# A decoder trunk on one core: the value projection of the first mixer with 512 moving columns in two goes, in place of 256 in four

## The chip, the cores and the metric

The kernel runs on one core of a Trainium2 chip. The metric is the device time of one launch in microseconds (us), taken as the median of several runs; a difference of about 0.2% (2.5 us here) is what a measurement of this kernel can tell from no change. Engines are named as in the profile: PE is the matrix engine's matmul side and PEld its weight loads, DVE is the vector engine, ACT the scalar engine, POOL the general engine, SP the engine that issues most transfers.

## The reference

A two-layer decoder trunk over 512 tokens and a model width of 1024, all in float32. Layer 0 is a gated linear recurrence (the *first mixer* below), layer 1 differential attention; each is followed by a gated convolutional FFN. Only the first mixer is touched:

```
def hgrn2_mixer(h, w_in, w_out, g_norm, lb):
    proj = h @ w_in
    q, f, i, g = jnp.split(proj, [HG_FDIM, 2 * HG_FDIM, 3 * HG_FDIM], axis=-1)
    q = jax.nn.silu(q)
    log_f = jnp.logaddexp(jnp.log(lb), jnp.log1p(-lb) + jax.nn.log_sigmoid(f.astype(jnp.float32)))
    k = -jnp.expm1(log_f)
    ...
    def step(S, blk):
        qb, kb, vb, lfb = blk
        b = jnp.cumsum(lfb, axis=1)
        o_inter = jnp.einsum('bthk,bhkv->bthv', qb * jnp.exp(b), S)
        scores = jnp.einsum('bthk,bshk,btshk->bhts', qb, kb, decay)
        o_intra = jnp.einsum('bhts,bshv->bthv', scores, vb)
        S_new = jnp.exp(b_last)[..., None] * S + jnp.einsum('bshk,bshv->bhkv', k_dec, vb)
        return S_new, o_inter + o_intra
    ...
    o = rmsnorm(o, g_norm) * jax.nn.silu(g.astype(jnp.float32))
    return (o @ w_out).astype(h.dtype)
```

There are eight heads of width 128. The projections q, f and g are wanted channel by token; the values i (here *values*, V) are wanted token by channel, since they are summed over tokens.

## The kernel before, in words

**Products.** A float32 product is made as three matmuls of operands that are split into a high and a low part (`mm3`, L99, L100, L101). For q, f and g the weights stand in the array and 512 tokens move: eight steps of the inner dimension, so 24 matmuls of 512 columns for each head and projection. For the values the tokens stand in the array (a block of 128) and the weights move: `value` (L279). Weights come as tiles of 128 x 1024 (512 KB): `stage` (L81) lets SP transfer one into one of three buffers `wst`; `split` makes the high part on ACT (L59) and the low part on DVE (L60), into one of three pairs `whi`, `wlo`. `spare` is a fourth such pair, used later in the mixer for the output projection.

**Values before.** The 1024 value columns are made in four goes of 256, each for two heads. A go takes two weight tiles, each holding 4 steps of the inner dimension by 256 columns, and four token blocks: 4 x 8 x 3 = 96 matmuls of 256 columns. ACT moves each of the four results from PSUM into a tile `vt` of 128 x 4 x 256 (L331), of which there are two. The first go is begun in the hand-ordered opening (`begin`): the first token block whole and the second by half.

**Per head.** `prep(h)` (L334 on) turns the projections f and q into decayed queries and keys at six block sizes, on DVE and ACT. The six key tiles of a head share one set of six buffers (`KB`), so the first of them for the next head (`k1`, L346) must wait until the matmuls that read this head's `k1` are done. `intra(h)` (L416) then has these pieces on PE: *part one*, 64 small matmuls that make scores of 32-token blocks (L423, L425), further scores (L430, L434, L437) and three transposes (L445); `kv`, three products of keys and values (L450); and the *output products* (L490, L492), which read the values `vt` and the assembled scores `scd`. Between part one and the output products DVE puts the scores into place with masked copies (L468, L479), ACT copies them into `scd` (L482, L485, L487), and DVE makes the running state `S` (L454). `gate` and `readout` follow for an earlier head.

**Order.** Outside the opening no order is written by hand in this mixer: the framework lists the instructions of each engine by its own estimate when the program is built, and each engine then runs its list in that order. PSUM has four banks called `mm` (projections and values) and four called `at` (the pieces of `intra`).

Of the kernel before, what the change touches and what calls it, by code (L numbers as in the profile page):

```python
# [11 lines left out]
F32 = mybir.dt.float32  # L12
F32R = mybir.dt.float32r
I32 = mybir.dt.int32
AF = mybir.ActivationFunctionType
# [4 lines left out]
P = 128  # L20
T = 512
D = 1024
KD = D // P
NH = 8
# [12 lines left out]
class Trunk:  # L37
# [192 lines left out]
    def begin(self, xs, acc, products, raw):  # L230

        tc, nc, a = self.tc, self.nc, self.a
        v, s = nc.vector, nc.scalar
        parts = [self.weight_tiles() for _ in products]
        for k in range(KD):
            nc.sync.dma_start(self.x[k], a["x_t"][k])
            if k in PIECES:
                c = slice(k * P, PIECES[k] * P)
                nc.sync.dma_start(raw[:, :, c], a["w_fqg"][0:len(products), :, c].rearrange("n p k -> p n k"))
        staged = [self.stage(a["w_i"][0, n]) for n in range(2)]  # L240
        sqs = [acc] + [self.sp.tile([P, T], F32, tag="sq", name="sq", bufs=2) for _ in range(KD - 1)]
        tail = range(max(PIECES), KD)

        def add(n):
            v.tensor_tensor(acc, acc, sqs[n], ALU.add)

        with tc.manual_schedule(engines=ORDERED):
            warm = self.bank("at")
            for _ in range(WARM):
                nc.tensor.matmul(warm[:, 0:P], self.ones, self.ones, start=True, stop=True)  # L250
            for k in range(KD):
                xs.append(self.x_split(k, 0))
                if k in PIECES:
                    c = slice(k * P, PIECES[k] * P)
                    for n, (hi, lo) in enumerate(parts):
                        self.split(raw[:, n, c], hi[:, c], lo[:, c])
                if k < tail[0]:
                    for ps, w in zip(products, parts):
                        self.proj(ps, w, xs, [k])
                s.activation(sqs[k], self.x[k], AF.Square)  # L260
                if k > 1:
                    add(k - 1)
                if k == KD - 3:
                    self.setup_rest()
            add(KD - 1)
            proj_tail = lambda n: self.proj(products[n], parts[n], xs, tail)
            ws = []
            for n in range(2):
                proj_tail(n)
                ws.append(self.weight_split(staged[n]))  # L270
            rc = self.rms(self.sums(acc, "at"), "n0")
            proj_tail(2)
            values = [self.bank("mm"), self.bank("at")]
            self.value(values[0], xs, ws, 0, range(KD))
            self.value(values[1], xs, ws, 1, range(KD // 2))
            rb = self.rows(rc, "n0", "at")
        return rb, rc, ws, values

    def value(self, ps, xs, ws, j, ks):  # L279

        tk = slice(j * P, (j + 1) * P)
        for k in ks:
            hi, lo = ws[k // 4]
            c = slice((k % 4) * 256, (k % 4) * 256 + 256)
            self.mm3(ps[:, :256], (xs[k][0][:, tk], xs[k][1][:, tk]), (hi[:, c], lo[:, c]), k == 0, k == KD - 1)

    def hgrn(self, xs, acc, on_tile):
        tc, nc, a, sp = self.tc, self.nc, self.a, self.sp
        v, s = nc.vector, nc.scalar
        with ExitStack() as ctx:  # L290
            hp = ctx.enter_context(tc.tile_pool(name="hgrn", bufs=1))
# [3 lines left out]
            spare = [hp.tile([P, 1024], F32R, tag=f"spare{i}", name=f"spare{i}") for i in range(2)]  # L295
# [24 lines left out]
                self.proj(ps, w, xs, range(KD))  # L320
                return ps

            def values(qt):
                ws = w_i if qt == 0 else [self.weights(a["w_i"][qt, n]) for n in range(2)]
                vt = hp.tile([P, 4, 256], F32, tag="vt", name="vt", bufs=2)
                for j in range(4):
                    ps, ks = self.bank("mm") if qt or j > 1 else begun[j], range(KD)
                    if qt == 0 and j < 2:
                        ks = range(KD // 2, KD) if j else ()
                    self.value(ps, xs, ws, j, ks)  # L330
                    s.activation(vt[:, j], ps[:, :256], AF.Identity, scale=rc[:, j:j + 1])  # L331
                return vt

            def prep(h, f_ps, q_ps):  # L334
# [81 lines left out]
            def intra(h, vt, r1, r2, qs, ks, tt):  # L416
                mm = nc.tensor.matmul
# [20 lines left out]
                       qs[64][:, P * c + 64:P * c + 128], start=True, stop=True, tile_position=(0, 0))  # L438

                ch = lambda t, c: t[:, c * P:(c + 1) * P]  # L440
                vh = lambda j: vt[:, j, (h % 2) * P:(h % 2 + 1) * P]
                q128, k128 = qs[128], ks[128]
                pk = self.bank("at")
                for c in range(3):
# [58 lines left out]
            def keep(h, po):  # L503
                o = big("o", "o", 2)
                self.sq_add(oacc, po, h == 0)
                s.copy(o, po)
                return o
# [7 lines left out]
            for h in range(NH):  # L515
                if h:
                    f_ps, q_ps = project(3 * h), project(3 * h + 1)
                if h == 0:
                    gate0 = gate(0, g_ps)
                pr[h] = prep(h, f_ps, q_ps)  # L520
                if h % 2 == 0:
                    vt[h // 2] = values(h // 2)
                if h:
                    o[h - 1] = keep(h - 1, intra(h - 1, vt[(h - 1) // 2], *pr.pop(h - 1)))
                if h > 1:
                    readout(h - 2, o[h - 2], gate(h - 2, project(3 * h - 4)) if h > 2 else gate0)
                if h == 2:
                    self.bias_vector()
            gg = [gate(h, project(3 * h + 2)) for h in (NH - 2, NH - 1)]
            readout(NH - 2, o[NH - 2], gg[0])  # L530
            o[NH - 1] = keep(NH - 1, intra(NH - 1, vt[3], *pr.pop(NH - 1)))
            readout(NH - 1, o[NH - 1], gg[1])
            steps, got = self.norm_steps(oacc, "o", "at")
            self.residual(a["w_ao"], ys, KD, on_tile, lambda: got[1][0], [None] * 3 + [spare], between=steps,
# [670 lines left out]
def by_quarter(w):  # L1205
    return np.ascontiguousarray(w.reshape(2, 4, P, 4, 256).transpose(3, 0, 2, 1, 4).reshape(4, 2, P, 1024))


def score_mask():

    s = np.arange(P) % 32
    m = np.zeros((P, 144), np.int32)
    kinds = [("q", 0), ("q", 1), ("q", 2), ("q", 3), (1, 0), (2, 0), (2, 1), (3, 0), (3, 2), (3, 1)]
    for y, (i, g) in enumerate(kinds):
        for n in range(8):
            if i == "q":
                m[:, y * 8 + n] = s == 4 * n + g
            else:
                m[:, y * 8 + n] = s == 4 * n + i - 1 - g
    kinds = [(1, 0), (2, 0), (3, 0), (2, 1), (3, 1), (3, 2)]  # L1220
    for y, (i, g) in enumerate(kinds):
        for n in range(2):
            m[:, 80 + y * 8 + n * 4:80 + y * 8 + n * 4 + 4] = (s // 4 == 4 * n + i - 1 - g)[:, None]
    m[:, 128:144] = (s < 16)[:, None]
    return m
# [19 lines left out]
def pack(i):  # L1245
    hot, far = t5_buckets()
    i = {k: np.asarray(v) for k, v in i.items()}
    w_in = i["a_w_in"][0]
    q, f, iv, g = (w_in[:, n * D:(n + 1) * D] for n in range(4))
    fqg = np.stack([by_tile(f), by_tile(q), by_tile(g)], 1).reshape(24, P, D)  # L1250
    d = {
        "x_t": np.ascontiguousarray(i["x"][0].T).reshape(KD, P, T),
        "w_fqg": fqg,
        "w_i": by_quarter(iv),
        "w_ao": by_tile(i["a_w_out"][0]),
        "gains": np.stack([columns(t) for t in (i["norm_mix"][0], i["norm_ffn"][0], i["kv_norm"], i["norm_mix"][1],
                                                i["norm_ffn"][1], i["final_norm"], i["a_gnorm"][0])], 1),
        "pack": np.concatenate([
            np.eye(P, dtype=np.float32), columns(i["a_lb_logits"][0]), columns(i["a_lb_logits"][1]),
            i["ffn_conv_w"].reshape(2, 3, 2 * KF, P).transpose(3, 0, 1, 2).reshape(P, -1),  # L1260
            i["ffn_conv_b"].reshape(2, 2 * KF, P).transpose(2, 0, 1).reshape(P, -1),
            i["b_subln"][0].reshape(P, 1)], 1),
        "rel": np.concatenate([i["rel_table"], hot], 1),
        "lam": np.stack([i[k][0] for k in ("b_lam_q1", "b_lam_k1", "b_lam_q2", "b_lam_k2")], 1),
        "w_up": np.stack([by_tile(w).reshape(2, KF, P, D).transpose(1, 0, 2, 3).reshape(2 * KF, P, D)
                          for w in i["ffn_w_up"]]),
        "w_down": np.stack([by_tile(w) for w in i["ffn_w_down"]]),
        "w_kq": np.stack([by_tile(i["kv_w"][:, :D]), by_tile(i["b_w_q"][0])], 1).reshape(16, P, D),
        "w_v": by_quarter(i["kv_w"][:, D:]),
        "w_o": by_tile(i["b_w_o"][0]),  # L1270
        "c_far": far,
        "c_mask": score_mask(),
    }
    return d
# [16 lines left out]
```

## Time and profile before

| | |
|---|---|
| median of 3 runs | 1240.84 us (1240.6 to 1240.98) |
| the profiled execution | 1240.69 us, of which the span of its instructions is 1238.4 us |
| busy in the span | PE 99%, PEld 84%, DVE 68%, ACT 47%, POOL 1% |
| the first mixer | about 24 us to 257 us of the span |
| value matmuls, first mixer | 384 of 128x256, eight transfers of 512 KB of `w_i` |

A busy time counts an instruction from its start to its modelled end; matmuls overlap, so their pace is read from the distance of their starts, not from their durations. "idle before <-X" is time in which an engine stood still and the last event that ended it.

### The profile page before, as it was taken

The page shows a single profiled execution, that of the slowest core. Times are in us where ns is not written, and L with a number is a line of the kernel's source. Part 1 is how long each engine was busy: PE and PEld are TensorE (multiplying, and loading weights), DVE is VectorE, ACT ScalarE, POOL GpSimd, SP SyncE. Part 2 cuts the span into 40 slices and gives each one's busy share as a digit, 9 for nine tenths or more (in the row PEclk, how much of TensorE's full clock was granted, in tenths as well). Part 3 has the DMA queues.
Part 4 walks back from the last instruction along what each step waited for, and adds up shares of the span by engine and source line. Part 5 has one row for each costly group of instructions (what it writes and reads, how often), then busy time and mean ns, then how long its engine had stood idle before and what let it go on. Part 6 is the DMA issues. An engine that isn't in the chain of part 4 may idle for free.

```text
span 1238.4 us, 18006 instructions
## 1 busy us (share of the span) xinstructions
PE 1227.0 (99%) x6994; PEld 1040.1 (84%) x6994; DVE 840.8 (68%) x1643; ACT 578.0 (47%) x1007; POOL 10.0 (1%) x32
## 2 busy tenths in 40 slices
PE   9999999999999999999999999999999999999997
PEld 8888898888888888888888989888888888888886
DVE  6988889587777777633356787877687777762333
ACT  6564555454444444422355666655444444442223
POOL 0000000000000000000000000000000000000001
PEclk9999999999999999999999999999999999999999
DMA  6234222232333333333333322313233333323322
GB/s 233 69 86 123 86 79 60 69 119 86 102 98 89 102 101 88 92 94 97 105 88 115 91 74 79 105 65 90 85 102 102 89 98 102 91 88 96 101 85 69
DMA packets 39613, 117.46 MB, mean 95 GB/s; under 512 B 4280, under 2 KB 10216, under 8 KB 39528
## 3 DMA queue, kind: packets, MB, share of 16 engines
q1 hardware_dynamic: 38488, 115.37, 31.0%
q8 instruction: 55, 0.90, 0.3%
q10 hardware_dynamic: 1040, 0.94, 0.2%
q14 instruction: 30, 0.25, 0.1%
HBM read 112.09 MB, written 3.68 MB: 93 GB/s over the span
## 4 chain that ended last, share of the span: by engine, by line
PE 96%; DVE 1%; ACT 1%; DMA 0%; issue 0%; SPq 0%; ACTq 0%; DVEq 0%
PE mm L99 28%; PE mm L100 28%; PE mm L101 28%; PE po L1020 1%; PE sc L977 1%; PE sc L99 1%; PE sc L100 1%; PE sc L976 1%; PE sc L101 1%; PE tp L1007 1%; PE at L490 1%; PE at L423 1%; PE at L492 0%; PE at L450 0%; DMA raw<-in_w_fqg_dram 0%; PE at L437 0%
## 5 line engine op out<-in xcount | busy, mean ns | idle before, releaser
L99 PE MATMUL mm<-xh,whi 128*128 128x512 f32 x944 | 370.8, 393 | 0.4 <-ACT whi L59 0.3
L100 PE MATMUL mm<-xl,whi 128*128 128x512 f32 x944 | 368.7, 391 | 0.5 <-DVE xl L63 0.5
L101 PE MATMUL mm<-xh,wlo 128*128 128x512 f32 x944 | 367.8, 390 | 0.0
L60 DVE TENSOR_TENSOR wlo<-wst,whi 128x1024 fp32r<-128x1024 f32 (+1 forms) x172 | 206.4, 1203 | 142.8 <-ACT whi L59 140.8
L59 ACT CAST whi<-wst 128x1024 fp32r<-128x1024 f32 (+1 forms) x172 | 177.1, 1033 | 244.5 <-PE mm L100 208.3
L99 PEld LDWEIGHTS mm<-xh,whi 128*128 128x128 f32 x944 | 177.4, 188 | 37.4 <-ACT whi L59 0.9
L101 PEld LDWEIGHTS mm<-xh,wlo 128*128 128x128 f32 x944 | 177.2, 188 | 37.0 <-DVE wlo L60 0.2
L100 PEld LDWEIGHTS mm<-xl,whi 128*128 128x128 f32 x944 | 177.4, 188 | 36.8 <-DVE xl L63 2.0
L99 PE MATMUL mm<-hh,whi 128*128 128x512 f32 (+1 forms) x374 | 141.0, 377 | 0.0
L100 PE MATMUL mm<-hl,whi 128*128 128x512 f32 (+1 forms) x374 | 140.8, 377 | 0.0
L101 PE MATMUL mm<-hh,wlo 128*128 128x512 f32 (+1 forms) x374 | 140.8, 376 | 0.0
L679 DVE TENSOR_TENSOR u<-mm,rbc_f 128x512 f32<-128x512 f32 x88 | 60.2, 688 | 73.4 <-PE mm L101 73.4
L101 PEld LDWEIGHTS mm<-hh,wlo 128*128 128x128 f32 x374 | 70.4, 188 | 13.0
L100 PEld LDWEIGHTS mm<-hl,whi 128*128 128x128 f32 x374 | 70.4, 188 | 12.9
L99 PEld LDWEIGHTS mm<-hh,whi 128*128 128x128 f32 x374 | 70.4, 188 | 12.8
L59 ACT CAST hh<-c 128x512 fp32r<-128x512 f32 x44 | 27.3, 620 | 102.7 <-DVE c L690 102.7
L681 ACT ACTIVATE c<-u,pack 128x512 f32<-128x512 f32 x88 | 71.5, 817 | 7.7 <-DVE u L679 3.6
L99 PE MATMUL mm<-whi,xh 128*128 128x256 f32 x248 | 71.6, 289 | 0.0
L101 PE MATMUL mm<-whi,xl 128*128 128x256 f32 x248 | 70.2, 283 | 0.0
L100 PE MATMUL mm<-wlo,xh 128*128 128x256 f32 x248 | 70.1, 283 | 0.0
L683 DVE SCALAR_TENSOR_TENSOR c<-u,pack,c 128x512 f32<-128x512 f32 x88 | 66.1, 751 | 2.7
L682 DVE SCALAR_TENSOR_TENSOR c<-u,pack,c 128x512 f32<-128x512 f32 x88 | 65.4, 745 | 0.0
(283 smaller groups left out, 1689.0 us busy)
## 6 DMA issues: line engine op xcount, KB each, us to landing
wst<-in_w_up_dram SPq DMA_DIRECT2D x88, 512.0 KB, 3.6
wst<-in_w_down_dram SPq DMA_DIRECT2D x32, 512.0 KB, 3.5
wst<-in_w_fqg_dram SPq DMA_DIRECT2D x21, 512.0 KB, 3.7
wst<-in_w_kq_dram SPq DMA_DIRECT2D x16, 512.0 KB, 3.6
wst<-in_w_down_dram SPq DMA_DIRECT2D x16, 384.0 KB, 3.1
wst<-in_w_i_dram SPq DMA_DIRECT2D x8, 512.0 KB, 3.7
wst<-in_w_ao_dram SPq DMA_DIRECT2D x8, 512.0 KB, 4.5
wst<-in_w_v_dram SPq DMA_DIRECT2D x8, 512.0 KB, 3.6
```

The source lines that it names most:

```text
L59: i = nc.scalar.copy(hi, x)
L60: j = nc.vector.tensor_tensor(lo, x, hi.bitcast(F32), ALU.subtract)
L99: mm(out, s[0], m[0], start=start, stop=False)
L100: mm(out, s[0], m[1], start=False, stop=False)
L101: mm(out, s[1], m[0], start=False, stop=stop)
L423: mm(pa[row, c * P:c * P + 80], ks[1][:, st], r1[:, :, 8 * bk:8 * bk + 8], start=True, stop=True, tile_position=(0, 32 * g))
L490: mm(ch(po, j), vh(j), sct[:, j], start=True, stop=(j == 0))
L679: v.tensor_tensor(u[:, 2:], ps, rb, ALU.mult)
L681: s.activation(c, u[:, 2:], AF.Identity, bias=self.cb[:, layer, n:n + 1], scale=w(2))
L682: v.scalar_tensor_tensor(c, u[:, 1:T + 1], w(1), c, ALU.mult, ALU.add)
L683: v.scalar_tensor_tensor(c, u[:, 0:T], w(0), c, ALU.mult, ALU.add)
L976: mm(sc[c], qs[h][:, c, oi], ks[h][0][:, c, 0:n], start=True, stop=False)
```

## The change

Values are made in two goes of 512 columns, each for four heads. A go takes four weight tiles, each with 2 steps of the inner dimension by 512 columns, and 4 x 8 x 3 = 96 matmuls of 512 columns. The fourth weight pair of a go is `spare`. `vt` becomes 128 x 4 x 512 with one buffer in place of two of 256 (the same bytes). In the opening the first two token blocks are each begun by half. In the loop over heads, `values` now comes behind `intra` of the head before, and for heads 0 and 4 in place of 0, 2, 4 and 6. The host lays `w_i` out by halves; the bytes are the same.

```
             values = [self.bank("mm"), self.bank("at")]
-            self.value(values[0], xs, ws, 0, range(KD))
-            self.value(values[1], xs, ws, 1, range(KD // 2))
+            for j in range(2):
+                self.value(values[j], xs, ws, j, range(KD // 2))
             rb = self.rows(rc, "n0", "at")
...
         tk = slice(j * P, (j + 1) * P)
         for k in ks:
-            hi, lo = ws[k // 4]
-            c = slice((k % 4) * 256, (k % 4) * 256 + 256)
-            self.mm3(ps[:, :256], (xs[k][0][:, tk], xs[k][1][:, tk]), (hi[:, c], lo[:, c]), k == 0, k == KD - 1)
+            hi, lo = ws[k // 2]
+            c = slice(k % 2 * T, k % 2 * T + T)
+            self.mm3(ps, (xs[k][0][:, tk], xs[k][1][:, tk]), (hi[:, c], lo[:, c]), k == 0, k == KD - 1)
...
-            def values(qt):
-                ws = w_i if qt == 0 else [self.weights(a["w_i"][qt, n]) for n in range(2)]
-                vt = hp.tile([P, 4, 256], F32, tag="vt", name="vt", bufs=2)
+            def values(half):
+                ws = w_i if half == 0 else []
+                for n in range(len(ws), 4):
+                    ws.append(self.weights(a["w_i"][half, n], tiles=spare if n == 3 else None))
+                vt = hp.tile([P, 4, T], F32, tag="vt", name="vt")
                 for j in range(4):
-                    ps, ks = self.bank("mm") if qt or j > 1 else begun[j], range(KD)
-                    if qt == 0 and j < 2:
-                        ks = range(KD // 2, KD) if j else ()
-                    self.value(ps, xs, ws, j, ks)
-                    s.activation(vt[:, j], ps[:, :256], AF.Identity, scale=rc[:, j:j + 1])
+                    begun_j = half == 0 and j < 2
+                    ps = begun[j] if begun_j else self.bank("mm")
+                    self.value(ps, xs, ws, j, range(KD // 2 if begun_j else 0, KD))
+                    s.activation(vt[:, j], ps, AF.Identity, scale=rc[:, j:j + 1])
                 return vt
...
-                if h % 2 == 0:
-                    vt[h // 2] = values(h // 2)
                 if h:
-                    o[h - 1] = keep(h - 1, intra(h - 1, vt[(h - 1) // 2], *pr.pop(h - 1)))
+                    o[h - 1] = keep(h - 1, intra(h - 1, vt[(h - 1) // 4], *pr.pop(h - 1)))
+                if h % 4 == 0:
+                    vt[h // 4] = values(h // 4)
```

The lists that the framework makes of this move too. At head 3 PE's list has, between the last transposes of part one and the output products, before the change three projections in a row (the q, f and g matmuls have the token tile `xh` or `xl` first, the value matmuls the weight tile):

```order
L445 MATMUL at_1752<-pack_247,k128_1281 128x128 x3
L99 MATMUL mm_1803<-xh0_141,whi_1799 128x512
...
L450 MATMUL at_1758<-vt_924,kt_1756 128x128 x3
...
L99 MATMUL mm_1844<-xh0_141,whi_1840 128x512
...
L99 MATMUL mm_1875<-xh0_141,whi_1871 128x512
...
L490 MATMUL at_1784<-scd1_377,vt_924 128x128 x2
L492 MATMUL at_1784<-q128_1280,S_1762 128x128
```

These are 22 matmuls of 512 ahead of `kv` and 45 behind it. With the change the same place reads:

```order
L446 MATMUL at_1528<-pack_247,k128_1174 128x128 x3
L99 MATMUL mm_1674<-whi_1587,xh4_217 128x512
...
L101 MATMUL mm_1674<-spare0_96,xl7_264 128x512
L451 MATMUL at_1534<-vt_464,kt_1532 128x128 x3
L491 MATMUL at_1560<-scd1_365,vt_464 128x128 x2
L493 MATMUL at_1560<-q128_1173,S_1538 128x128
...
L426 MATMUL at_1878<-r2_1421,k4_1417 32x48
L99 MATMUL mm_1706<-xh0_141,whi_1702 128x512
```

Twelve matmuls of the second go's last token block stand ahead of `kv`, and none between `kv` and the output products; the next projections (`mm_1706`, 72 matmuls) come behind them and behind 18 matmuls of part one of head 4. ACT's list at that place is now:

```order
L486 COPY scd1_365<-at_1499 32x4x32 x2
L488 COPY scd1_365<-at_1499 64x4x64
L332 ACTIVATE vt_1595<-mm_1596,rcol_n0_297 128x512
L332 ACTIVATE vt_1595<-mm_1622,rcol_n0_297 128x512
L332 ACTIVATE vt_1595<-mm_1648,rcol_n0_297 128x512
L332 ACTIVATE vt_1595<-mm_1674,rcol_n0_297 128x512
L143 ACTIVATE sq_1569<-at_1560 128x512
```

The second go's four results leave PSUM together, behind the `scd` copies of head 3; before, each go's four results were spread around such copies, into the other of the two `vt` buffers. From the end of the mixer on, the lists of all engines are the same as before.

More of the change, by code (lines that the diff above doesn't have):

```diff
@@ L440, in intra @@
                 ch = lambda t, c: t[:, c * P:(c + 1) * P]
-                vh = lambda j: vt[:, j, (h % 2) * P:(h % 2 + 1) * P]
+                vh = lambda j: vt[:, j, h % 4 * P:(h % 4 + 1) * P]
                 q128, k128 = qs[128], ks[128]
@@ L530, in hgrn @@
             readout(NH - 2, o[NH - 2], gg[0])
-            o[NH - 1] = keep(NH - 1, intra(NH - 1, vt[3], *pr.pop(NH - 1)))
+            o[NH - 1] = keep(NH - 1, intra(NH - 1, vt[1], *pr.pop(NH - 1)))
             readout(NH - 1, o[NH - 1], gg[1])
@@ L1206, in by_quarter, with by_half @@
     return np.ascontiguousarray(w.reshape(2, 4, P, 4, 256).transpose(3, 0, 2, 1, 4).reshape(4, 2, P, 1024))
+def by_half(w):
+    return np.ascontiguousarray(w.reshape(4, 2, P, 2, T).transpose(3, 0, 2, 1, 4).reshape(2, 4, P, 1024))
 def score_mask():
@@ L1253, in pack @@
         "w_fqg": fqg,
-        "w_i": by_quarter(iv),
+        "w_i": by_half(iv),
         "w_ao": by_tile(i["a_w_out"][0]),
```

## The prediction

> **What bounds the kernel now.** I began with the page's busy times and its chain of waits.
>
> ```profile
> PE 1227.0 (99%) x6994; PEld 1040.1 (84%) x6994; DVE 840.8 (68%) x1643; ACT 578.0 (47%) x1007; POOL 10.0 (1%) x32
> PE 96%; DVE 1%; ACT 1%; DMA 0%; issue 0%; SPq 0%; ACTq 0%; DVEq 0%
> ```
>
> PE carries the end: whatever shortens PE's list shortens the kernel, as long as no new wait opens. So the second view is the waits of PE in the first mixer (20 to 260 us), and the third the busy time of all engines there in stretches.
>
> ```profile
> PE at L490 <- issue: 1.3, 1, 1.3
> ...
> 30.00:60.00 30.00, 30.00 (x270) 25.67 (x268) 29.02 (x77) 15.46 (x31) 0.00 (x0) 1.00 0.24 71
> 120.00:150.00 30.00, 30.00 (x389) 26.46 (x388) 23.66 (x62) 18.77 (x42) 0.00 (x0) 1.00 0.25 76
> ```
>
> In the second kind of row the columns are PE, PEld, DVE, ACT, POOL, granted clock, DMA share and GB/s. PE stands still only once in the mixer, 1.3 us before output products (those of head 0). But DVE is busy 29 of 30 us at the start of the mixer and 24 of 30 later, and a head's output products need what DVE makes. PE is never late because its list always holds other matmuls while DVE works. That cover is what this change rearranges, so the order matters as much as the matmuls' price.
>
> **The price of the matmuls.** Their pace is read from starts in the timeline of PE.
>
> ```profile
> 24.23 0.29 PE L99 MATMUL mm<-whi,xh 128*128 128x256 f32 x1
> ...
> 29.51 0.28 PE L101 MATMUL at<-whi,xl 128*128 128x256 f32 x1
> ...
> 36.05 0.40 PE L100 MATMUL mm<-xl,whi 128*128 128x512 f32 x1
> ...
> 39.92 0.39 PE L99 MATMUL mm<-xh,whi 128*128 128x512 f32 x1
> ```
>
> From 24.23 to 29.51 lie 44 steps between value matmuls of 256 columns: 5.28 / 44 = 0.1200 us. From 36.05 to 39.92 lie 17 steps of 512: 3.87 / 17 = 0.2276 us. Two of 256 become one of 512: 0.2400 - 0.2276 = 0.0124 us saved, 192 times, **-2.4 us**. Single steps of the second run read 0.22 to 0.24, which bounds the term at -3.8 and 0. [...]
>
> ACT moves half as many results of twice the width; it is busy about half of the time here, so that is hidden but for the place below. Eight transfers of 512 KB stay eight, all on SP. In the opening the third and fourth weight tiles are now values too.
>
> ```profile
> 22.55 4.00 SPq L81 DMA_DIRECT2D wst<-in_w_fqg_dram  x3
> 23.88 1.05 ACT L59 CAST whi<-wst 128x1024 fp32r<-128x1024 f32 x1 [1.24 <-PE mm L100]
> 24.96 1.23 DVE L60 TENSOR_TENSOR wlo<-wst,whi 128x1024 fp32r<-128x1024 f32 x1 [0.20 <-ACT whi L59]
> DMA to landing us min/median/max: 3.6/3.7/4.1
> ...
> DMA to landing us min/median/max: 3.5/3.9/7.9
> ```
>
> The third tile is split by 26.2. The fourth is issued at 22.55, lands at most 4.1 later (the landings of 20 to 40 us) at 26.7, and is split by 26.7 + 1.05 + 1.23 = 29.0. The two first halves (24 matmuls of 0.2276 from 23.9) keep PE until 29.3, and the fourth tile is wanted after seven more. Nothing waits: **0**. If the landing took 7.9 us, the longest of the first 80, PE would wait some 2 us; this is kept for the upper end.
>
> **The wait that goes.** Before head 0's output products PE has had 31 matmuls of 512 and 73 of 256 since the transposes (15.8 us) and will have 67 of 512 (15.2 us). DVE's list in that stretch loses a weight split, `qe`, `F` and the sums that follow it, and gains four short products, about 3 us less by their usual durations (an estimate). The wait of 1.3 us should vanish: **-1.3**, or 0 at the other end.
>
> **The wait that comes.** The place is head 3, with the order shown above. These rows of PE, DVE and ACT are head 3 as it is before the change.
>
> ```profile
> 126.72 0.21 PE L425 MATMUL at<-r,k 128*32 128x48 f32 x1
> 128.02 0.55 PE L445 MATMUL at<-pack,k 128*128 128x128 f32 x3
> 128.32 0.48 PE L99 MATMUL mm<-xh,whi 128*128 128x512 f32 x1
> 133.41 0.83 PE L450 MATMUL at<-vt,kt 128*128 128x128 f32 x6
> 134.00 0.48 PE L100 MATMUL mm<-xl,whi 128*128 128x512 f32 x1
> 144.31 0.60 PE L490 MATMUL at<-scd,vt 128*128 128x128 f32 x4
> ...
> 127.15 0.48 DVE L346 TENSOR_SCALAR k<-sn,om 128x512 f32<-128x512 f32 x1
> 136.49 0.68 DVE L497 TENSOR_TENSOR ge<-mm,rbc_n 128x512 f32<-128x512 f32 x1
> 137.09 0.18 DVE L468 COPY_PREDICATED sd<-mask,at 128x32 f32<-128x32 int32 x1
> 137.45 1.22 DVE L60 TENSOR_TENSOR wlo<-wst,whi 128x1024 fp32r<-128x1024 f32 x1
> 138.58 0.17 DVE L468 COPY_PREDICATED sd<-mask,at 128x16 f32<-128x16 int32 x1
> 138.74 0.68 DVE L500 TENSOR_TENSOR gg<-ge,sg 128x512 f32<-128x512 f32 x1
> 139.34 0.22 DVE L479 COPY_PREDICATED sd<-mask,at 128x64 f32<-128x64 int32 x1
> ...
> 139.59 1.22 ACT L482 COPY scd<-sd 32x128 f32<-32x128 f32 x4 [1.74 <-DVE sd L479]
> 141.35 0.37 ACT L487 COPY scd<-at 64x256 f32<-64x256 f32 x1
> ...
> DVE k L346 <- PE at L425: 0.6, 1, 0.6
> ```
>
> Part one ends at 126.72. DVE's keys for head 4 may start only then (the last row is a wait of just that kind), and head 3's masked copies are strewn among them, in one list. DVE goes from 127.15 to the last copy at 139.34, ACT's `scd` copies take from 139.59 to 141.72, and the output products start at 144.31 without a wait, because 67 other matmuls stood between.
>
> With the change DVE's list there has the same operations less `ge` (137.09 - 136.49 = 0.60), `gg` (139.34 - 138.74 = 0.60) and one split (138.58 - 137.45 = 1.13), since no gate's projection can be made yet. Counted from the end of part one: 0.43 to `k1`, then 139.59 - 127.15 - 2.33 = 10.11, then 2.13 for the copies and 0.1 to PE, 12.8 us. PE covers 128.32 - 126.72 = 1.60, twelve matmuls (2.73) and `kv` (134.00 - 133.41 = 0.59), 4.9 us. PE cannot pass on: its list runs in order, and the projections behind need an `mm` bank. All four hold value results, which ACT may not move while head 3 still reads the only `vt`. So PE waits 12.8 - 4.9 = **+7.8 us**.
>
> Bounds of this term: with the whole 12.44 of before, +10.2. From below, the last head, where no keys of a next head are strewn in:
>
> ```profile
> 225.01 0.55 PE L445 MATMUL at<-pack,k 128*128 128x128 f32 x3
> ...
> 231.06 0.23 DVE L479 COPY_PREDICATED sd<-mask,at 128x64 f32<-128x64 int32 x1
> ...
> 233.09 0.36 ACT L487 COPY scd<-at 64x256 f32<-64x256 f32 x1
> ```
>
> There the copies end 8.4 us after the transposes begin; the transposes begin 1.3 after part one, so 9.8 - 4.9 = +4.9. I take 7.8, because the list of the change does hold head 4's keys.
>
> Behind the wait PE does its output products and 18 small matmuls, then needs a bank: ACT moves the first result only after the last read of `vt`.
>
> ```profile
> 145.42 0.39 PE L490 MATMUL at<-scd,vt 128*128 128x128 f32 x2
> 30.26 0.59 ACT L198 COPY rbc_n<-at 128x512 f32<-128x512 f32 x1
> ```
>
> The last read starts 1.1 after the first; with its own 0.4 and a move of about 0.6 the bank is free at 2.1, when PE has spent about 1.7 on those matmuls: **+0.4**, between 0 and 1.
>
> **The clock.** A wait of almost 8 us would be far longer than any in this trace, and its clock rows bear on what follows.
>
> ```profile
> 0.99 3.78 PE L250 MATMUL at<-ones 128*128 128x128 f32 x16 [0.99 <-POOL ones L212]
> 4.67 0.59 PE L99 MATMUL mm<-xh,whi 128*128 128x512 f32 x1
> 5.62 0.40 PE L101 MATMUL mm<-xh,wlo 128*128 128x512 f32 x1
> 1230.00:1233.60 3.60, 1.27 (x8) 0.94 (x8) 2.05 (x10) 1.18 (x4) 0.61 (x1) 1.00 0.41 139
> 1234.00:1238.00 4.00, 0.00 (x0) 0.00 (x0) 0.40 (x2) 0.00 (x0) 0.40 (x1) 0.50 0.79 262
> ```
>
> With PE thinly busy the granted clock fell to 0.50 within about 4 us, and from the first matmul at 0.99 it took until about 5 us before a 512 lasted 0.40 again. So I expect the clock to fall during the wait, and about 4 us at half pace behind it, which do 2 us of work: **+2.0**, between 0 and 2.3 (4.6 us at half pace). [...]
>
> **Elsewhere.** In heads 1 and 2 DVE is within 1 or 2 us of PE in the new order (by an estimate from the usual durations of the listed operations, some 18 and 14 us between part one and the last masked copy, against 22 and 17 us of PE), so 0, with up to +3 if it slips. From head 4 on, 67 to 74 matmuls stand between transposes and output products as before, 40 in the last head: 0. Behind the mixer the lists are unchanged.
>
> **The sum.** 1240.69 - 2.4 - 1.3 + 7.8 + 0.4 + 2.0 = 1247.2 for a profiled execution, whose span is 2.3 shorter; that execution stood 0.15 below the median, so **1247.3 us**.
>
> **Rivals.**
> *The clock stays up.* For it: the fall in the tail is the only one in this trace, and small matmuls stood before it. The same sum without 2.0: 1245.3.
> *DVE slips earlier.* DVE's 29 of 30 us speaks for it; against it, DVE has finished head 0's keys by the time that the longer first go ends, so it enters head 1 with little left over. The output products of heads 1 or 2 then wait too, up to 3 us: 1250.3.
> [...]
> *The change does what its words say and no more.* If head 3's blocks were ready when PE comes to them, as everywhere before, only the gains are left: 1240.84 - 3.7 = 1237.1. It needs 7.8 us of DVE work to vanish.
>
> **How the numbers follow.** Forecast 0.50, clock stays 0.22, DVE slips 0.14, short wait 0.08, gains only 0.06. The measurement tells 0.2%, 2.5 us, from no change: faster is below 1238.4, slower above 1243.3. Faster is the last case, 0.06; same is the short wait and a few hundredths of the clock's case where the wait is nearer 6, 0.12; slower the rest, 0.82. The range of 1242.0 to 1250.5 leaves out the last case, the far end of a slipping DVE, and little else. All upper bounds together would give 1240.84 + 10.2 + 1.0 + 2.3 = 1254.3 without the opening, all lower ones 1240.84 - 3.8 - 1.3 + 4.9 = 1240.6; neither set comes together.
>
> **What would show it.** Value matmuls at steps near 0.2276, 192 of them. One idle stretch of 7 to 8 us before output products around 137 us, with the `scd` copies as what ends it, and DVE busy with `k`, `q` and masked copies in it. A granted clock under 1.00 in the 5 us behind it. No wait of PE at 70 us nor in the opening. The forecast is wrong if that idle stretch is under 5 us, if PE's other waits in the mixer come to more than 2 us, or if a 512 of values steps by 0.24 or more.

## The result, and the profile after

The changed kernel takes **1249.22 us** (median of 4 runs, 1248.95 to 1249.45) against 1240.73 for the kernel before on the same chip: a ratio of **1.0067, 95% interval 1.0055 to 1.0079**, slower by 8.5 us. The forecast was 1247.3, with a range of 1242.0 to 1250.5. The profiled execution took 1249.26 us, of which the span is 1247.5.

The page's busy times and chain of the changed kernel, and PE's waits in the first mixer (columns: us in total, times, longest):

```profile
PE 1228.6 (98%) x6802; PEld 1033.0 (83%) x6802; DVE 840.8 (67%) x1643; ACT 577.1 (46%) x999; POOL 10.0 (1%) x32
PE 90%; DVE 6%; ACT 2%; issue 1%; DMA 0%; SPq 0%; ACTq 0%; DVEq 0%
```

```profile
PE at L491 <- ACT scd L488: 8.9, 3, 7.6
```

The chain now runs through DVE and ACT for 8% of the span: 90% of it is PE, where it was 96%. (This share does not measure the wait: the run below that fills the wait with matmuls has the very same line.) The 1.3 us wait of before is gone; in its place are three waits at output products (their line is L491 now, since the lines from about 330 on stand one line further down), and one of them has almost all of the time. PE's list shows where:

```profile
131.71 0.21 PE L426 MATMUL at<-r,k 128*32 128x48 f32 x1
...
136.13 0.83 PE L451 MATMUL at<-vt,kt 128*128 128x128 f32 x6
144.54 1.23 PE L491 MATMUL at<-scd,vt 128*128 128x128 f32 x4 [7.58 <-ACT scd L488]
...
206.02 0.71 PE L491 MATMUL at<-scd,vt 128*128 128x128 f32 x4 [0.49 <-ACT scd L488]
...
229.41 0.71 PE L491 MATMUL at<-scd,vt 128*128 128x128 f32 x4 [0.85 <-ACT scd L488]
```

Part one of head 3 ends at 131.71. PE does its small matmuls, the last twelve matmuls of the values and `kv`, and stands still for 7.58 us before head 3's output products. The two small waits are heads 5 and 6. What DVE and ACT did meanwhile in head 3:

```profile
132.11 0.48 DVE L347 TENSOR_SCALAR k<-sn,om 128x512 f32<-128x512 f32 x1
...
137.80 1.23 DVE L60 TENSOR_TENSOR wlo<-wst,whi 128x1024 fp32r<-128x1024 f32 x1
...
142.10 0.23 DVE L480 COPY_PREDICATED sd<-mask,at 128x64 f32<-128x64 int32 x1
```

```profile
142.36 1.22 ACT L483 COPY scd<-sd 32x128 f32<-32x128 f32 x4 [1.13 <-DVE sd L480]
...
144.12 0.36 ACT L488 COPY scd<-at 64x256 f32<-64x256 f32 x1
```

DVE goes from head 4's keys at 132.11 to head 3's last masked copy at 142.10 without a break, ACT copies until 144.48, and PE goes on at 144.54: 12.8 us from the end of part one.

The clock granted around that wait and the engines' busy time in the two stretches shown of before (columns as there: PE, PEld, DVE, ACT, POOL, clock, DMA share, GB/s):

```profile
136.00:139.80 3.80, 0.96 (x8) 0.73 (x6) 3.80 (x14) 2.10 (x7) 0.00 (x0) 1.00 0.01 2
139.90:150.00 10.10, 5.46 (x52) 5.03 (x53) 2.36 (x12) 5.24 (x14) 0.00 (x0) 0.50 0.17 54
150.10:153.00 2.90, 2.90 (x14) 2.38 (x14) 0.69 (x1) 0.80 (x2) 0.00 (x0) 1.00 0.00 0
...
30.00:60.00 30.00, 30.00 (x243) 24.55 (x241) 23.32 (x57) 15.41 (x26) 0.00 (x0) 1.00 0.29 88
120.00:150.00 30.00, 22.42 (x248) 19.49 (x247) 18.33 (x64) 16.55 (x41) 0.00 (x0) 0.83 0.26 84
```

The granted clock falls to 0.50 at 139.83, while PE waits, and comes back to 1.00 only at 150.07: PE works 5.5 us at half pace behind the wait (two output products take 0.43 us there by their starts, and 0.22 in the same trace at 186 us, where the granted clock is 1.00). In the opening stretch DVE is busy 23.3 us of 30, where it was 29.0.

The pace of the new value matmuls, in PE's timeline in the opening:

```profile
42.24 0.39 PE L99 MATMUL mm<-whi,xh 128*128 128x512 f32 x1
...
44.74 0.39 PE L101 MATMUL mm<-whi,xl 128*128 128x512 f32 x1
```

Eleven steps in 2.50 us, 0.2273 each.

All of the loss lies in the first mixer. The sums behind its last head (L178), of the kernel before and of the changed one:

```profile
242.02 0.95 PE L178 MATMUL at<-ones,oacc 128*128 128x1 f32 x8
```

```profile
251.09 0.95 PE L178 MATMUL at<-ones,oacc 128*128 128x1 f32 x8
```

They stand 9.07 us later, and the span is 9.1 us longer (1247.5 against 1238.4). The time of the two profiled executions differs by 8.6 only, since what lies outside the span is 1.8 us in the one and 2.3 in the other.

### The profile page after: what moved, and what is told of

Same layout as the page of the kernel before. It is cut to its first block, busy times and chain, and to the rows that moved or that the text cites. A ratio compares the mean times of both kernels' runs of the same rounds, so it can differ in the third digit from the quotient of the medians.

```text
span 1247.5 us, 17615 instructions
## 1 busy us (share of the span) xinstructions
PE 1228.6 (98%) x6802; PEld 1033.0 (83%) x6802; DVE 840.8 (67%) x1643; ACT 577.1 (46%) x999; POOL 10.0 (1%) x32
## 4 chain that ended last, share of the span: by engine, by line
PE 90%; DVE 6%; ACT 2%; issue 1%; DMA 0%; SPq 0%; ACTq 0%; DVEq 0%
PE mm L99 27%; PE mm L100 27%; PE mm L101 27%; PE po L1021 1%; DVE wlo L60 1%; PE sc L978 1%; PE sc L99 1%; PE sc L100 1%; PE sc L977 1%; PE sc L101 1%; DVE sd L469 1%; PE tp L1008 1%; PE at L491 0%; PE at L99 0%; PE at L101 0%
## 5 line engine op out<-in xcount | busy, mean ns | idle before, releaser
L60 DVE TENSOR_TENSOR wlo<-wst,whi 128x1024 fp32r<-128x1024 f32 x170 | 203.8, 1202 | 141.4 <-ACT whi L59 139.2
L59 ACT CAST whi<-wst 128x1024 fp32r<-128x1024 f32 x170 | 175.0, 1033 | 255.7 <-PE mm L100 220.4
L101 PEld LDWEIGHTS mm<-hh,wlo 128*128 128x128 f32 x374 | 70.4, 188 | 12.8
L689 ACT ACTIVATE c<-c 128x512 f32<-128x512 f32 x44 | 27.8, 632 | 74.4 <-DVE c L684 74.3
L99 PE MATMUL mm<-whi,xh 128*128 128x256 f32 (+1 forms) x170 | 54.1, 318 | 0.0
L100 PE MATMUL mm<-wlo,xh 128*128 128x256 f32 (+1 forms) x170 | 52.6, 309 | 0.0
```

What stands on the lines that cost most here:

```text
L59: i = nc.scalar.copy(hi, x)
L60: j = nc.vector.tensor_tensor(lo, x, hi.bitcast(F32), ALU.subtract)
L99: mm(out, s[0], m[0], start=start, stop=False)
L100: mm(out, s[0], m[1], start=False, stop=False)
L101: mm(out, s[1], m[0], start=False, stop=stop)
L689: s.activation(cg, cg, AF.Silu)
```

## The experiments

The theory: head 3's output products wait because all four `mm` banks hold value results which cannot be moved while head 3 still reads the only `vt`, so PE has no projection to do meanwhile; behind the wait the clock is at half. The rivals: the 512 columns or their longer goes are dear in themselves; the half clock costs nothing that the wait has not cost already. Each ratio is against runs of the kernel before on the same chip.

### What the half clock costs

The order of everything is kept; behind the products of keys and values of head 3, 30 matmuls are put into PE's finished list, whose results go into the bank of the transposes, which nobody reads any more.

```
...
+            i, bank = block.instructions[place[product]], block.instructions[place[transpose]].outs
+            for m in range(30):
+                block.instructions.insert(place[product] + 1, copy.replace(i, name=f"I-{10 ** 6 + m}", outs=bank, sync_info=None))
...
+    fill_behind(nc, TR[3], KV[3])
```

> The change with 30 matmuls more, which compute nothing that is used: they stand behind head 3's products of keys and values, in the stretch in which TensorE only waits, and write into a bank that nobody reads any more. The order of all else is the same. They take 30 x 0.215 = 6.4 of the 7.6 us; the copies that head 3's output products wait for still end at the same time. My theory (the wait lets the clock fall, and half pace for 5.5 us behind it costs 2.8 us of its own): the granted clock stays at 1.00, the output products start when they did, and the kernel ends 2.8 us sooner: 1246.4 (1246.0 to 1247.0). Rival (the half clock is only shown, or DVE's and ACT's work hides it, and the wait is all): 1249.2 within 0.4.

Measured: 1246.73 us, ratio 1.0047 (1.0033 to 1.0061), 2.5 us under the changed kernel's 1249.22. PE's timeline, and the clock in that stretch:

```profile
136.35 7.53 PE L451 MATMUL at<-vt,kt 128*128 128x128 f32 x66
144.78 0.71 PE L491 MATMUL at<-scd,vt 128*128 128x128 f32 x4 [0.90 <-ACT scd L488]
...
248.77 0.95 PE L178 MATMUL at<-ones,oacc 128*128 128x1 f32 x8
```

```profile
136.00:153.00 17.00, 16.10 (x144) 14.66 (x143) 7.19 (x26) 8.66 (x22) 0.00 (x0) 1.00 0.09 32
```

The output products start when they did (144.78, in a kernel that began its values 0.2 us later), since DVE and ACT set that time. But the granted clock stays at 1.00, and from those products to the sums behind the last head PE needs 248.77 - 144.78 = 103.99 us, where it was 251.09 - 144.54 = 106.55. The half clock behind the wait costs **2.6 us** of its own. The two ratios' intervals overlap a little; the two traces settle it, as their lists differ in nothing else.

### One buffer, without the 512 columns

The kernel before, with goes of 256 columns; only its second buffer is taken away:

```
-                vt = hp.tile([P, 4, 256], F32, tag="vt", name="vt", bufs=2)
+                vt = hp.tile([P, 4, 256], F32, tag="vt", name="vt", bufs=1)
```

> The kernel before, with goes of 256 columns, and only one buffer for the values in place of two. The values of the next two heads can then be moved only when the earlier two are done, at heads 1, 3 and 5, and the order has no matmul at all between the transposes and the output products of these three heads. My theory (one buffer holds all four banks, and the cover is lost, whatever the width): three waits of 7 to 10.4 us, each with 2.8 us of half clock and 0.4 for the bank behind it: 1240.7 + 3 x (10.2 to 13.6) = 1271 to 1282. Rival A (the loss needs the 512 columns or the longer goes): 1240 to 1244.

Measured: 1280.15 us, ratio 1.0318 (1.0304 to 1.0332). Three such waits of PE, in its timeline:

```profile
90.88 1.19 PE L490 MATMUL at<-scd,vt 128*128 128x128 f32 x4 [9.83 <-issue]
...
153.43 0.80 PE L490 MATMUL at<-scd,vt 128*128 128x128 f32 x2 [9.03 <-ACT scd L487]
...
220.11 1.22 PE L490 MATMUL at<-scd,vt 128*128 128x128 f32 x4 [9.04 <-ACT scd L487]
```

27.9 us of waiting, in heads 1, 3 and 5. (For the first the profile names no releaser; ACT's `scd` copies end at 90.78, 0.10 us before it ends.) Of the other 11.4 us, 6.2 are the half clock (12.4 us at half pace behind the three waits, by the trace's record of the clock) and 2.4 are short waits ahead of `kv`, which has lost its cover too; 2.8 I did not assign. The wait needs no 512 columns: it came at each of the three places where four results stand in the four banks behind a buffer that is still read.

### More cover, the buffer still alone

The second go is emitted behind the gate's projection of head 2:

```
-                if h % 4 == 0:
-                    vt[h // 4] = values(h // 4)
+                if h == 0:
+                    vt[0] = values(0)
                 if h > 1:
                     readout(h - 2, o[h - 2], gate(h - 2, project(3 * h - 4)) if h > 2 else gate0)
+                if h == 4:
+                    vt[1] = values(1)
```

> The change with the second go of the values emitted behind the gate's projection of head 2 in place of before it. Still one buffer and 512 columns. 31 matmuls of 512 stand between head 3's transposes and its output products in place of 12, nine of them behind the products of keys and values. My theory (the wait is DVE's and ACT's 12.8 us from the end of part one less what TensorE still has to do): 1.6 + 31 x 0.2276 + 0.6 = 9.3 us of cover, a wait of 3.5 us in place of 7.6; 1249.2 - 4.1 = 1245.1, and 1242.3 if so short a wait leaves the clock up. Rival A (the loss comes with the 512 columns or the goes, not with the missing cover): 1249.2 within 1.

Measured: 1247.59 us, ratio 1.0055 (1.0042 to 1.0069). Faster than the change by 1.6 us, but not by 4. PE and DVE in head 3:

```profile
149.86 1.22 PE L491 MATMUL at<-scd,vt 128*128 128x128 f32 x4 [6.53 <-ACT scd L488]
```

```profile
137.70 0.68 DVE L60 TENSOR_TENSOR y<-y,y 128x512 fp32r<-128x512 f32 x1
...
141.90 1.22 DVE L60 TENSOR_TENSOR wlo<-wst,whi 128x1024 fp32r<-128x1024 f32 x1
...
143.81 1.22 DVE L60 TENSOR_TENSOR wlo<-wst,whi 128x1024 fp32r<-128x1024 f32 x1
...
145.73 1.22 DVE L60 TENSOR_TENSOR wlo<-wst,whi 128x1024 fp32r<-128x1024 f32 x1
```

The cover was there (PE stood still from 143.3, 9.6 us behind part one), but the chain of DVE and ACT had grown with it: from part one's end at 133.7 to 149.86 it took 16.1 us in place of 12.8. Two more weight splits and the split of `y` now stood among head 3's masked copies (2 x 1.13 + 0.60 = 2.9 us by the distance of starts). The wait is chain less cover, as the theory has it; that the chain would keep its length was an assumption, and it failed. The half clock behind the wait lasted 3.6 us here, 1.9 us less than in the change, and costs about 0.9 less; with the 1.05 us of wait saved this makes 1.9. From the first value matmul to the sums behind the last head the two traces differ by 2.2 (24.94 to 249.81 against 24.06 to 251.09). The medians differ by 1.6 only; the openings, in which the first value matmul comes between 23.8 and 25.1 us in the ten traces, spread by as much as is missing.

### The buffer cut into eight

```
-                vt = hp.tile([P, 4, T], F32, tag="vt", name="vt")
+                tiles = [hp.tile([P, 256], F32, tag="vt", name="vt", bufs=8) for _ in range(8)]
+                vt = [tiles[j::4] if half == 0 else tiles[2 * j:2 * j + 2] for j in range(4)]
...
-                    s.activation(vt[:, j], ps, AF.Identity, scale=rc[:, j:j + 1])
+                    for n in range(2):
+                        s.activation(vt[j][n], ps[:, n * 256:n * 256 + 256], AF.Identity, scale=rc[:, j:j + 1])
...
-                vh = lambda j: vt[:, j, h % 4 * P:(h % 4 + 1) * P]
+                vh = lambda j: vt[j][h % 4 // 2][:, h % 2 * P:(h % 2 + 1) * P]
```

> The change with one thing altered: the buffer for the values is cut into eight tiles of 256 columns, one for each token block and pair of heads, so that a result of the second go needs only tiles of its own two pairs. Tiles of the first pair of heads have been free since head 1. Same 192 value matmuls of 512 columns at the same place; two moves of 256 in place of one of 512. My theory (the wait at head 3 comes from the one buffer, which holds all four banks): two banks come free at once, 56 matmuls stand between head 3's transposes and its output products in place of 12, the wait of 7.6 us and the fall of the clock go, and what is left are the gains: 1240.7 - 2.4 - 1.3 = 1237.0, with up to 1 us more since the last head has 32 matmuls there in place of 40: 1236.5 to 1238.5. Rival A (the loss comes with the 512 columns or with the place of the values behind the earlier head, whatever the buffer): it stays within 1 us of 1249.2. Rival B (512 columns gain nothing on the chip, only the wait matters): 1239.5 to 1241.

Measured: 1243.54 us, ratio 1.0024 (1.0014 to 1.0033): 5.7 us better than the change, and 6.5 worse than expected. PE's waits:

```profile
PE at L493 <- ACT scd L490: 3.9, 2, 3.4
PE at L453 <- ACT kt L450: 1.0, 1, 1.0
```

Head 3 no longer waits at all. But heads 5 and 6 do, 4.8 us in all, and behind the longest, 3.40 us, the granted clock is at 0.50 once more. Rows of PE, DVE and ACT in head 6:

```profile
201.66 0.21 PE L428 MATMUL at<-r,k 128*32 128x48 f32 x1
...
222.95 1.22 PE L493 MATMUL at<-scd,vt 128*128 128x128 f32 x4 [3.40 <-ACT scd L490]
...
199.44 0.55 DVE L346 TENSOR_SCALAR F<-sf,om,lb 128x512 f32<-128x512 f32 x1 [1.11 <-ACT sf L343]
...
207.07 0.49 DVE L349 TENSOR_SCALAR k<-sn,om 128x512 f32<-128x512 f32 x1
...
218.63 0.23 DVE L482 COPY_PREDICATED sd<-mask,at 128x64 f32<-128x64 int32 x1
...
218.81 1.05 ACT L59 CAST whi<-wst 128x1024 fp32r<-128x1024 f32 x1
219.82 1.04 ACT L59 CAST spare<-wst 128x1024 fp32r<-128x1024 f32 x1
220.78 1.21 ACT L485 COPY scd<-sd 32x128 f32<-32x128 f32 x4
```

```profile
175.00:200.00 25.00, 24.54 (x231) 20.48 (x230) 23.61 (x62) 13.77 (x31) 0.00 (x0) 1.00 0.24 81
200.00:225.00 25.00, 20.63 (x207) 17.21 (x207) 23.57 (x62) 13.67 (x30) 0.00 (x0) 0.96 0.24 79
222.80:226.10 3.30, 3.15 (x14) 3.06 (x14) 2.52 (x4) 2.29 (x4) 0.00 (x0) 0.50 0.77 293
```

Part one of head 6 ends at 201.66, and DVE could make the next keys from then on, but it comes to them only at 207.07: it has run without a break since 199.44. ACT adds two weight casts ahead of the copies, which so begin 1.9 us behind the last masked copy (218.86 to 220.78). The same 175 to 225 us in the kernel before:

```profile
175.00:200.00 25.00, 25.00 (x252) 22.10 (x251) 18.40 (x48) 12.87 (x28) 0.00 (x0) 1.00 0.26 75
200.00:225.00 25.00, 25.00 (x343) 21.11 (x341) 23.59 (x62) 14.94 (x32) 0.17 (x3) 1.00 0.30 87
```

There DVE is busy 18.4 of the first 25 us, and catches up while PE works on the 96 value matmuls of the last go (168.4 to 180.1), for which DVE only makes two splits. With both goes at 512 columns these matmuls have all been done before head 4, and DVE is busy 23.6 of 25 us in both stretches. This was a second cause that my theory lacked, so the next runs are about it.

The change itself has it too, without those casts. Its head 6:

```profile
210.14 0.21 PE L426 MATMUL at<-r,k 128*32 128x48 f32 x1
...
214.99 0.48 DVE L347 TENSOR_SCALAR k<-sn,om 128x512 f32<-128x512 f32 x1
...
227.23 1.22 ACT L483 COPY scd<-sd 32x128 f32<-32x128 f32 x4
```

In heads 5 and 6 of the change DVE comes to the next keys 4.2 and 4.9 us after part one; in the kernel before it is 1.7 us in both. ACT's copies follow the last masked copy within 0.03 us, and PE waits 0.49 and 0.85 us. With eight tiles DVE is hardly later (3.0 and 5.4 us). That head 6 waits so much longer there has two other sources in that run's new lists: the casts (1.9 us), and less work for PE between part one and the output products (16.9 us, in the change 18.4).

### Relief for DVE in the late heads

The kernel with eight tiles, with F and the first keys of heads 5 to 7 made by ACT:

```
+                if h > 4:
+                    s.activation(F, sf, AF.Identity, bias=lb[:, h:h + 1], scale=om[:, h:h + 1])
+                else:
                     v.tensor_scalar(F, sf, om[:, h:h + 1], lb[:, h:h + 1], ALU.mult, ALU.add)
...
+                if h > 4:
+                    s.activation(ks[1], sn, AF.Identity, scale=om[:, h:h + 1])
+                else:
                     v.tensor_scalar(ks[1], sn, om[:, h:h + 1], None, ALU.mult)
```

> The run with eight tiles (1243.5 us), with two of DVE's products per head (the gate F and the keys, 0.55 and 0.49 us) done by ACT instead in heads 5, 6 and 7. Nothing else is edited, though the order around them may shift. My theory (in heads 5 and 6 DVE is what TensorE waits for, since these heads have no value matmuls to work under): DVE gets 1 us per head back, about 2 to 3 us over the heads up to the last wait, and the waits of 5.5 us in all shrink as much: 1240.5 to 1241.5. Rival A (those waits are ACT's weight casts ahead of the copies, or the order alone): ACT has 1 us more per head to do, 1243.5 or more. Rival B (the lateness is worth nothing): 1243.5 within 0.5.

Measured: 1239.05 us, ratio 0.9986 (0.9978 to 0.9995); 4.5 us better than without. The waits left in PE's list:

```profile
PE at L499 <- ACT scd L496: 2.1, 2, 1.3
```

2.7 us of waiting went, as forecast, and with the long wait the fall of the clock (1.00 from 200 to 225 us, where it was 0.96), some 1.6 us by half of the 3.3 us at half pace, an estimate, which the expectation had left out. But that DVE's relief alone did this is not shown, since ACT's list has changed as well. In head 6 the casts now stand behind the copies:

```profile
216.00 1.22 ACT L491 COPY scd<-sd 32x128 f32<-32x128 f32 x4
...
218.67 1.04 ACT L59 CAST whi<-wst 128x1024 fp32r<-128x1024 f32 x1
```

The copies begin 0.26 us behind the last masked copy in place of 1.92, which is 1.7 us, half of the wait that head 6 had. DVE's share there is that its last masked copy ends 16.4 us after part one in place of 17.2. No run separates the two, so the rival of the casts is not excluded.

The control, the same edit on the kernel before:

> The kernel before, goes of 256 columns and two buffers, with the same two products of heads 5, 6 and 7 done by ACT. A control: it shows whether ACT's help is a gain by itself. My theory (TensorE waits for DVE in heads 5 and 6 only where these have no value matmuls): 1240.8 within 0.6, no difference. Rival (DVE's relief is worth its 3 us anywhere, and the run with eight tiles was no better than the kernel before for another reason): 1238 to 1239.

Measured: 1240.65 us, ratio 1.0000 (0.9991 to 1.0009). The same edit is worth nothing where the late heads have value matmuls, and 4.5 us where they have none. It takes away waits that the kernel before has not got; how much of that is DVE's relief and how much ACT's new order, the control does not tell.

The same help from head 3 on (the line stands at two places):

```
-                if h > 4:
+                if h > 2:
```

> The run with eight tiles and ACT's help (1239.05 us), with ACT making F and the keys from head 3 on in place of head 5 on. Two waits of 0.85 and 1.27 us were left there, in heads 5 and 6. My theory (these are what DVE is still late): 2 us of DVE's work more go away ahead of them, the waits shrink to under 0.5 in all, and both goes at 512 columns then give the whole gain of 2.4 + 1.3: 1237.0 to 1238.0. Rival (what is left there is ACT's own work, casts of weights ahead of the copies): 1239 or more.

Measured: 1238.82 us, ratio 0.9984 (0.9975 to 0.9992); waits of 1.6 us are left, at the same two places. 2 us of DVE's work less took only 0.5 us off the waits, and 0.2 off the time. The rival does not hold either: at both places ACT begins the `scd` copies 0.26 us behind the last masked copy, with no cast between. What the trace shows in head 6 is the keys, now ACT's, 3.5 us after part one (199.29):

```profile
202.23 0.63 ACT L358 ACTIVATE sq__2406<-qe 128x512 f32<-128x512 f32 x1 [1.87 <-DVE qe L357]
202.77 0.71 ACT L353 ACTIVATE k<-sn,om 128x512 f32<-128x512 f32 x1
```

ACT's list has them behind an activation (`sq_`) that waited 1.87 us for DVE's `qe`, so DVE's lateness reaches them all the same. No run takes this order away.

### One wide go, two narrow ones

Heads 0 to 3 get a go of 512 columns; heads 4 and 5, and 6 and 7, get goes of 256 at their old places, and `vt` is two buffers of 256 again.

```
-                vt = hp.tile([P, 4, T], F32, tag="vt", name="vt")
+                vt = [hp.tile([P, 4, 256], F32, tag="vt", name="vt", bufs=2) for _ in range(pairs)]
...
-                if h % 4 == 0:
-                    vt[h // 4] = values(h // 4)
+                if h in (0, 4, 6):
+                    vt += values(h, 1 if h else 2)
+                if h:
+                    o[h - 1] = keep(h - 1, intra(h - 1, vt[(h - 1) // 2], *pr.pop(h - 1)))
...
```

> Only the first go is 512 columns wide (heads 0 to 3, with the spare weight pair); heads 4 and 5, and then 6 and 7, get goes of 256 columns at the places of the kernel before, and the values lie in the two buffers of the kernel before. So 96 matmuls of 512 take the place of 192 of 256, no go needs a buffer that is still read, and two goes stand in the later heads again. My theory (the loss is the lost cover at head 3 and, as the run with eight tiles showed, DVE's lateness in heads 5 and 6, which have no value matmuls any more): no wait at head 3, none in heads 5 and 6, none at head 0: 1240.84 - 96 x 0.0124 (1.2) - 1.3 = 1238.3 (1237.5 to 1239.5), faster than the kernel before. Rival A (the longer first go itself makes DVE late in the later heads): waits in heads 4 to 6 and 1240 to 1244. Rival B (the 512 columns gain nothing): 1239.5 to 1240.8.

Measured: **1237.65 us, ratio 0.9973 (0.9963 to 0.9983)**, faster than both kernels. In its list PE waits for nothing from 21 us to the end of the mixer, and where the change waited it is busy throughout:

```profile
120.00:150.00 30.00, 30.00 (x271) 26.08 (x271) 26.36 (x77) 18.64 (x42) 0.00 (x0) 1.00 0.33 99
200.00:225.00 25.00, 25.00 (x340) 21.42 (x331) 23.80 (x58) 15.16 (x32) 0.17 (x3) 1.00 0.30 89
```

It has half of the gain in matmuls, all of the wait at head 0, and none of the two losses. With value matmuls in the later heads again DVE comes to the keys 1.7 and 1.8 us after part one of heads 5 and 6, as in the kernel before. The two gains are 2.5 us of the 3.1; the other 0.6 I did not assign.

## Why the prediction was right, and where it was not

- **The price of the matmuls** (-2.4) held: 0.2400 - 0.2273 = 0.0127 us a pair, 192 times 2.4 us.
- **The wait that goes** (-1.3) held, and the opening waits for nothing new.
- **The wait that comes** (+7.8) held in place, size and releaser: 7.58 us, a chain of 12.8 us, as forecast, less a cover of 5.25 (131.71 to 136.96), forecast 4.9. That the banks behind the single buffer take the cover away is shown from two sides: it comes back without the 512 columns when a buffer is taken from the kernel before, and it is gone when the buffer is cut up. The **bank behind it** (+0.4) was at most 0.2: with the clock up, the projection starts at 147.32, right behind part one's first matmuls.
- **The clock** (+2.0, 0 to 2.3) fell during the wait and stayed at 0.50 behind it, as forecast, but the size was too small: 2.6 us by the run with 30 more matmuls, beyond the upper bound. The term took the 4 us of the start and of the tail; the clock came back only 5.5 us after PE did.
- **Elsewhere** (0 from head 4 on) is the step that failed. It counted the matmuls between transposes and output products, which are as many as before, but not that DVE comes to heads 5 and 6 later, once no value matmuls are left to work under. In the change this cost 0.49 + 0.85 us. With the stop at head 3 removed the same heads waited 4.8 us and the clock fell, but not because DVE was much later: the rest came with that run's new lists, ACT's casts ahead of the copies and less cover. Heads 1 and 2, where I had put the chance of DVE slipping, did not wait, but head 1 had only 0.5 us to spare (the copies end at 100.58, the output products start at 101.09).
- **The sum.** Of 9.1 us in the span, -2.4 - 1.3 + 7.6 + 2.6 + 1.3 and 0.2 of a later start of the values (24.06 against 23.87) are 8.0. Of the other 1.1 us, about 0.7 lies in the steps between small matmuls, by their starts in the traces: part one now stands directly behind output products four times, and its first start comes 0.2 us after their last, where a projection's came after 0.03. I had no term for it, and the last 0.4 I did not assign.

Of the rivals, *the clock stays up* fell with the granted clock of 0.50 and its 2.6 us. *A short wait*, the bound of 4.9 us, fell because DVE did head 4's keys among head 3's copies. To count it under *same* takes the clock as staying up, which no run shows for a wait of 4.9 us: with eight tiles the clock was at 0.50 behind 3.40. *Gains only* fell with the banks; the kernel with one wide go shows that it needs both losses gone.

## What to carry to other kernels

Before goes are merged, ask which buffer each result waits for, and how many banks the waiting results hold: the cover of every other engine's chain may be the projections that need those banks. Matmuls that want nothing from a busy engine are cover wherever they stand, so moving them forward leaves the later stages without; widen the go only where that engine has time to spare. When one loss is taken away the lists are made anew, and can bring waits of their own, as in heads 5 and 6 with eight tiles: read the new list of every engine, not only that of the one that you relieved, before the cause is named or the gain is counted.

## What the runs showed of the hardware

How long the half clock lasted differed from run to run. The trace's record of the granted clock has it at 0.50 for 10.24 us in the change (from 139.83), for 6.83 in the run with the later go (from 146.63) and for 3.41 in the one with eight tiles (from 222.79). PE had stood still from 136.96, 143.33 and 219.56 on, so the fall came 2.9 to 3.3 us into these waits, and PE worked at half pace for 5.5, 3.6 and 3.3 us behind them. The three long waits of the run with one narrow buffer had 10.24 us each, from 2.0 to 4.0 us into the wait on (the mean granted clock was 0.85 from 65 to 100 us, 0.91 from 130 to 150, 0.87 from 150 to 175 and 0.80 from 200 to 225). With eight tiles PE was back 0.16 us after the fall, 3.40 us of waiting having been enough. Around the wait of 1.3 us at head 0 of the kernel before (70 to 72 us) the granted clock was 1.00, and so it was around the last two waits, 1.3 us and less, of the run with ACT's help (175 to 225 us).

At the start the full pace came at different times behind the same first matmul. PE's first matmul starts at 0.99 us in both kernels' traces. A 512 first lasts 0.40 us at 5.62 in the kernel before; in the changed kernel it lasts 0.80 at 4.88 and 5.48, and 0.40 first at 6.83.

What such a stall costs beside itself was measured once: 2.6 us for 5.5 us at half pace, by the run with 30 more matmuls. Half of the time at half pace gives 2.8, 1.8 and 1.6 us for the change, the later go and the eight tiles, an estimate from the stretches above, where I had put 2.0 and at most 2.3. Why the clock came back sooner behind one wait than behind another, no run shows.
